# Hybrid SSD and attention layer: the first chunk's x and B transposed by TensorE instead of VectorE and DRAM

## The chip, the cores and the metric

The kernel runs on one core of a Trainium2 chip. The metric is device time in microseconds of one execution. The core's engines are TensorE (PE, with its weight loads as PEld), VectorE (DVE), ScalarE (ACT), GpSimd (POOL) and SyncE (SP); each works through its own queue of instructions in order and waits on semaphores set by the others. SyncE computes nothing here: it issues DMAs, in order too, and a DMA that has to wait holds back all that stand behind it.

## The reference

One decoder layer on 512 tokens of width 1024, in float32: a token mixer (a Mamba-2 SSD branch and a sliding-window attention branch from one input projection, merged by gates) and a SwiGLU FFN, with a layer norm around each. The change touches the chunked scan of the SSD branch alone. It has 32 heads of 64 in 4 groups of 8 heads, a state of 128, and 4 chunks of 128 tokens:

```python
X = (xh.astype(jnp.float32) * dt[..., None]).reshape(bsz, nc, T, ng, ne, hp)
Lmat = jnp.exp(segsum(dA))
CB = jnp.einsum('bclgn,bcsgn->bcgls', Cc, Bc)
y_diag = jnp.einsum('bcgels,bcsgep->bclgep', Lmat * CB[:, :, :, None], X)
decay_states = jnp.exp(a_cum[..., -1:] - a_cum)
states = jnp.einsum('bclgn,bcgel,bclgep->bcgepn', Bc, decay_states, X)
...
y_off = jnp.einsum('bclgn,bcgepn,bcgel->bclgep', Cc, h_in, jnp.exp(a_cum))
```

So each chunk needs X (x times dt), the decayed copy of X for the state, the state itself (B times decayed X, summed over the chunk's tokens), and two contributions to y: the diagonal one from L, CB and X, and the one from the state carried in.

## The kernel before

**Order.** TensorE's instructions stand in the order in which the code issues them (the schedule of TensorE is manual). Those of the other engines and the DMAs are put into their queues by a scheduler, so an edit can change their order at some distance. Pools give tiles a fixed number of buffers; an instruction that writes a tile whose buffer is still read waits.

**Products.** Every weight product is done in three matmuls per step of the contraction (`mm3`, L149 to L151): high times high, high times low, low times high. A weight tile arrives by DMA as `w_raw` (L120, four buffers), ScalarE rounds it to `w_hi` (L135) and VectorE makes the rest `w_lo` (L136), three buffers each, prepared up to three products ahead. A projection (`product`, L277) is 8 steps, 24 matmuls, into one of three PSUM accumulators `ps_mm`. It is a generator; `fill(us)` issues as many steps of the waiting generators as fit `us` at 0.65 us a step, with at most one step owed from before, and nothing when none is waiting.

**Stages.** First the input norm, and the projections of the attention branch with steps of others filled in; then attention; then products of the attention output. From 237 us the SSD stage runs: 16 turns i, four groups g of four chunks c. Its fill is the input projections of the next group (`g_xbc`, L357): a product, then a causal convolution in `evac`, one ScalarE instruction (L370) and three on VectorE (L373) that read the accumulator, then SiLU on ScalarE (L377).

**A turn of the SSD stage.** Everything lies with channels on the partitions, while X and B for the state are needed with tokens on the partitions.
- `ssd_pre(i)` (L739): SyncE loads the cumulative decays of the chunk from DRAM, broadcast to all partitions, into `L` (512 KB, three buffers, L745) and, for c > 0, `E` (L752). GpSimd masks L (L756) and ScalarE takes eight exponentials (L761).
- `ssd_x(i)` (L763): VectorE transposes x in blocks of 32 by 32 into `T` (four instructions, L770); SyncE writes T to DRAM (`t_d`, L774) and reads it back in the order that makes the transpose whole, into `R` (four DMAs, one buffer, L776). For c < 3 the same is done with B: `Tb` (one buffer, L781), `b_d` (L784), four reads into `bt` (L786).
- `ssd_dt(i)` (L790): VectorE multiplies R by dt into `X` (two instructions, L797), GpSimd multiplies X by the decays into `Xd` (two, L805).
- `ssd_a(i)` (L809): TensorE makes `ps_cb` from B and C (L822), ScalarE copies it to `cb` (L824), VectorE multiplies it into L (L826). At c = 0 ScalarE first writes `y_g` from x (four, L819).
- `ssd_b(i)` (L828): the state product `ps_st` from bt and Xd (L836), at c = 0 copied to `h_st` by ScalarE (L842), else added by VectorE (L848); for c > 0 the carried-in part `ps_yo` (L852); then, after a `fill`, the diagonal part `ps_yd` from X and L (L862), which VectorE adds to y (L864).

All PSUM tiles other than the three accumulators come from one pool of five buffers (`axt`).

**The start of the stage (L967 to L973).** Before the loop the code issues ssd_pre(0), ssd_pre(1), ssd_x(0), ssd_a(0), a fill, ssd_dt(0) and ssd_x(1). Turn 0 then adds the stage's projections to the fill queue (`add_stage`, L950) and issues ssd_pre(2), ssd_a(1), `fill(6.0)`, ps_st(0), ssd_dt(1), ssd_x(2), `fill(6.0)`, ps_yd(0), `fill(6.0)`.

Of the kernel before, what the change touches and what calls it, by code (L numbers as in the profile page):

```python
# [11 lines left out]
F32 = mybir.dt.float32  # L12
# [6 lines left out]
P = 128  # L19
# [43 lines left out]
def kernel(  # L63
# [13 lines left out]
    nc = tc.nc  # L77
# [3 lines left out]
    def pool(name, bufs=1, **kw):  # L81
        return tc.tile_pool(name=name, bufs=bufs, reuse_waits="tile", **kw)

    def gap(pl, size):
# [8 lines left out]
    ident = const.tile([P, P], F32, name="ident")  # L93
# [4 lines left out]
        out=tri, in_=tri, pattern=[[1, P]], compare_op=ALU.is_ge, fill=0.0,  # L98
# [54 lines left out]
    class Filler:  # L153
# [19 lines left out]
        def fill(self, us):  # L173
            self.owed += us / 0.65
            while self.owed >= 1.0 and self.step():
                self.owed -= 1.0
            self.owed = min(self.owed, 1.0)
# [91 lines left out]
    fill, need = filler.fill, filler.need  # L269

    def axt(shape, name):
        return psX.tile(shape, F32, name=name, tag="ax")

    def acc_tile(name):
        return psA.tile([P, S], F32, name=name, tag="mm")
# [79 lines left out]
    xbc_t = {}  # L355
# [184 lines left out]
    ps = [axt([P, S], "ps_dt"), axt([P, S], "ps_k"), acc_tile("ps_v"), acc_tile("ps_q")]  # L540
# [190 lines left out]
    sd = ssd_stack.enter_context(pool("ssd", side="right"))  # L731
# [5 lines left out]
    z_t, y_t, yn_t, L_t, E_t, R_t, X_t, Xd_t, bt_t, h_t = ({} for _ in range(10))  # L737

    def ssd_pre(i):  # L739

        g, c = divmod(i, NT)

        L = sd.tile([P, 2, 4, P], F32, name="L", tag="L", bufs=3)
        L_t[i] = L
        nc.sync.dma_start(  # L745
            out=L.rearrange("p j t l -> p j (t l)"),
            in_=ar[g, c].unsqueeze(0).broadcast_to([P, 2, 4 * P]))
        if c > 0:
            E = sd.tile([P, 4, P], F32, name="E", tag="E", bufs=2)
            E_t[i] = E  # L750
            for j in range(2):
                nc.sync.dma_start(  # L752
                    out=E[64 * j:64 * j + 64].rearrange("p t l -> p (t l)"),
                    in_=er[g, c, j].unsqueeze(0).broadcast_to([64, 4 * P]))
        Lf = L.rearrange("p j t l -> p (j t) l")
        nc.gpsimd.affine_select(  # L756
            out=Lf, in_=Lf, pattern=[[0, 8], [1, P]], compare_op=ALU.is_ge, fill=-BIG,
            base=0, channel_multiplier=-1)
        for j in range(2):
            for t in range(4):  # L760
                nc.scalar.activation(L[:, j, t], L[:, j, t], AF.Exp, bias=nac5[:, g, j, c, t:t + 1], scale=1.0)  # L761

    def ssd_x(i):  # L763

        g, c = divmod(i, NT)
        cs = slice(c * P, (c + 1) * P)

        T = sd.tile([P, 4, 4, 32], F32, name="T", tag="tmp", bufs=3)
        for t in range(4):
            nc.vector.transpose(T[:, :, t], xbc_t[g, 2 + t][:, cs])  # L770

        R = sd.tile([P, 4, 4, 32], F32, name="R", tag="R", bufs=1)
        R_t[i] = R
        nc.sync.dma_start(out=t_d[i], in_=T.rearrange("p b t s -> p b (t s)"))  # L774
        for b in range(4):
            nc.sync.dma_start(  # L776
                out=R[32 * b:32 * b + 32].rearrange("r a t s -> r a (t s)"),
                in_=t_d[i, :, b].rearrange("(a r) x -> r a x", r=32))
        if c < NT - 1:
            Tb = sd.tile([P, P], F32, name="Tb", tag="Tb", bufs=1)  # L780
            nc.vector.transpose(Tb, xbc_t[g, 0][:, cs])  # L781
            bt = sd.tile([P, P], F32, name="bt", tag="bt", bufs=2)
            bt_t[i] = bt
            nc.sync.dma_start(out=b_d[i], in_=Tb.rearrange("p (b s) -> p b s", b=4))  # L784
            for b in range(4):
                nc.sync.dma_start(  # L786
                    out=bt[32 * b:32 * b + 32].rearrange("r (a s) -> r a s", a=4),
                    in_=b_d[i, :, b].rearrange("(a r) s -> r a s", r=32))

    def ssd_dt(i):  # L790

        g, c = divmod(i, NT)
        R = R_t.pop(i)
        X = sd.tile([P, 4, 2, 64], F32, name="X", tag="X", bufs=2)
        X_t[i] = X
        for j in range(2):
            nc.vector.tensor_tensor(  # L797
                out=X[:, :, j].rearrange("p t (h s) -> p t h s", h=2),
                in0=R[:, 2 * j:2 * j + 2].rearrange("p h t s -> p t h s"),
                in1=dt5[:, g, j, c].unsqueeze(2).unsqueeze(3).broadcast_to([P, 4, 2, 32]), op=ALU.mult)  # L800
        if c < NT - 1:
            Xd = sd.tile([P, 4, 2, 64], F32, name="Xd", tag="Xd", bufs=1)
            Xd_t[i] = Xd
            for j in range(2):
                nc.gpsimd.tensor_tensor(  # L805
                    out=Xd[:, :, j], in0=X[:, :, j],
                    in1=dec5[:, g, j, c].unsqueeze(2).broadcast_to([P, 4, 64]), op=ALU.mult)

    def ssd_a(i):  # L809

        g, c = divmod(i, NT)
        cs = slice(c * P, (c + 1) * P)
        b_f, c_f = xbc_t[g, 0], xbc_t[g, 1]
        xs = [xbc_t[g, 2 + t] for t in range(4)]
        if c == 0:
            y = sd.tile([P, 4, S], F32, name="y_g", tag="y_g", bufs=1)
            y_t[g] = y
            for t in range(4):
                nc.scalar.mul(out=y[:, t], in_=xs[t], mul=pc[:, C_DS + 4 * g + t:C_DS + 4 * g + t + 1])  # L819
        L = L_t[i]  # L820
        ps = axt([P, P], "ps_cb")
        nc.tensor.matmul(ps, b_f[:, cs], c_f[:, cs], start=True, stop=True)  # L822
        cb = sd.tile([P, P], F32, name="cb", tag="cb", bufs=2)
        nc.scalar.copy(out=cb, in_=ps)  # L824
        Lf = L.rearrange("p j t l -> p (j t) l")
        nc.vector.tensor_tensor(out=Lf, in0=Lf, in1=cb.unsqueeze(1).broadcast_to([P, 8, P]), op=ALU.mult)  # L826
# [139 lines left out]

    ssd_pre(0)  # L967
    ssd_pre(1)
    ssd_x(0)
    ssd_a(0)  # L970
    fill(4.0)
    ssd_dt(0)
    ssd_x(1)  # L973
    norm = iter(())
    for i in range(NG * NT):
        g, c = divmod(i, NT)
# [13 lines left out]
        if i + 1 < NG * NT:  # L990
            ssd_dt(i + 1)
# [82 lines left out]
    for half in range(2):  # L1074
# [23 lines left out]
        for ti in toks:  # L1098
            hr = res[ti]
            for o in range(2):  # L1100
                os = slice(o * 512, (o + 1) * 512)
                nc.vector.scalar_tensor_tensor(
                    out=hr[:, os], in0=hr[:, os], scalar=ALPHA, in1=acc[ti][o], op0=ALU.mult, op1=ALU.add)
# [98 lines left out]
    for f in range(2, NF):  # L1202
        pss = []
        for u in (U_FG, U_FU):
            ps = psF.tile([P, S], F32, name="ps_ff", tag="mm")
# [23 lines left out]
    for cs in (slice(0, 256), slice(256, 512)):  # L1229
        ps = psD.tile([P, 256], F32, name="ps_end", tag="dn")  # L1230
# [74 lines left out]
```

## Time and profile before

| | |
|---|---|
| median of 3 runs | 1031.97 us (1031.74 to 1032.63) |
| the profiled execution | 1031.27 us |
| its span | 1029.5 us |
| TensorE busy | 1008.2 us, 98% of the span |
| VectorE, ScalarE, GpSimd busy | 616.8, 499.2, 207.4 us |
| mean granted clock of TensorE | 0.993 |

The span runs from the first to the last instruction; the rest of an execution's time lies around it. In rows of the timeline and of the chain the first two numbers are the start and the length in us; in brackets stands the idle time of the engine just before, and who ended it. Rows of the list of waits give total, count and longest. `x4` is a count of instructions. Matmuls overlap, so that a row's length is longer than the distance to the next start. A float32 matmul can be two records in the trace, hence `x2` at one ps_st and `x16` at the eight matmuls of one ps_yd.

### The profile page before, as it was taken

What the parts mean: (1) busy time and instruction counts of PE and PEld (TensorE: products, weight loads), DVE (VectorE), ACT (ScalarE), POOL (GpSimd) and SP (SyncE); (2) the same over time, 40 slices, a digit from 0 to 9 for tenths busy, and PEclk for the clock granted to TensorE, in tenths of its full rate; (3) what the DMA queues carried; (4) which work ended last, traced back from release to release, by engine and by line L of the source; (5) the groups of instructions that cost most, each with busy time, mean ns of one, the idle gap of its engine ahead of it and who ended that gap; (6) DMA issues with size and microseconds to landing.
All of it is one profiled execution on the core that took longest, in us unless ns stands there. A gap on an engine that the chain in (4) does not pass through costs nothing.

```text
span 1029.5 us, 13358 instructions
## 1 busy us (share of the span) xinstructions
PE 1008.2 (98%) x4968; PEld 830.0 (81%) x4968; DVE 616.8 (60%) x911; ACT 499.2 (48%) x848; POOL 207.4 (20%) x195
## 2 busy tenths in 40 slices
PE   8999999996999999999999999999999999999997
PEld 7888888884887887888888888898888888888886
DVE  6789874545655785696874585646433333332766
ACT  5464566716555786684652543334323332322441
POOL 2011223722204113212322820290000000000000
PEclk9999999998999999999999999999999999999999
DMA  8211223545554445445532344316433333331471
GB/s 316 82 62 62 88 83 106 198 146 148 171 156 146 153 153 151 125 142 159 166 113 83 115 150 180 107 42 225 144 122 114 111 111 114 123 123 62 147 251 53
DMA packets 58961, 136.53 MB, mean 133 GB/s; under 512 B 12912, under 2 KB 23152, under 8 KB 58640
## 3 DMA queue, kind: packets, MB, share of 16 engines
q1 hardware_dynamic: 56240, 126.11, 37.9%
q0 software_dynamic: 2080, 7.47, 2.0%
q10 hardware_dynamic: 576, 2.10, 0.5%
q8 instruction: 39, 0.64, 0.3%
q14 instruction: 26, 0.21, 0.1%
HBM read 124.25 MB, written 11.40 MB: 132 GB/s over the span
## 4 chain that ended last, share of the span: by engine, by line
PE 88%; DVE 4%; ACT 3%; DMA 3%; issue 1%; POOL 1%; SPq 0%; ACTq 0%; POOLq 0%; DVEq 0%
PE ps_mm L149 13%; PE ps_mm L150 13%; PE ps_mm L151 13%; PE ps_ff L151 8%; PE ps_ff L149 8%; PE ps_ff L150 8%; PE ps_da L151 2%; PE ps_da L149 2%; PE ps_da L150 2%; PE ps_db L150 2%; PE ps_db L151 2%; PE ps_db L149 2%; PE ps_mix L149 1%; PE ps_mix L151 1%; PE ps_mix L150 1%; DMA L<-a_d 1%
## 5 line engine op out<-in xcount | busy, mean ns | idle before, releaser
L136 DVE TENSOR_TENSOR w_lo<-w_raw,w_hi 128x1024 fp32r<-128x1024 f32 x185 | 241.3, 1309 | 171.1 <-ACT w_hi L135 169.0
L135 ACT CAST w_hi<-w_raw 128x1024 fp32r<-128x1024 f32 x185 | 193.6, 1050 | 307.9 <-PE ps_ff L150 124.4
L149 PE MATMUL ps_mm<-hT_hi,w_hi 128*128 128x512 f32 x504 | 204.3, 405 | 0.7 <-DVE cacc L373 0.7
L150 PE MATMUL ps_mm<-hT_lo,w_hi 128*128 128x512 f32 x504 | 197.2, 391 | 0.0
L151 PE MATMUL ps_mm<-hT_hi,w_lo 128*128 128x512 f32 x504 | 197.0, 391 | 0.0
L149 PE MATMUL ps_ff<-h2T_hi,w_hi 128*128 128x512 f32 (+1 forms) x384 | 143.3, 373 | 0.0
L151 PE MATMUL ps_ff<-h2T_hi,w_lo 128*128 128x512 f32 (+1 forms) x384 | 142.6, 371 | 0.0
L150 PE MATMUL ps_ff<-h2T_lo,w_hi 128*128 128x512 f32 (+1 forms) x384 | 142.6, 371 | 0.0
L149 PEld LDWEIGHTS ps_mm<-hT_hi,w_hi 128*128 128x128 f32 x504 | 95.0, 188 | 23.2 <-issue 4.2
L151 PEld LDWEIGHTS ps_mm<-hT_hi,w_lo 128*128 128x128 f32 x504 | 94.8, 188 | 20.6
L150 PEld LDWEIGHTS ps_mm<-hT_lo,w_hi 128*128 128x128 f32 x504 | 95.1, 189 | 18.7 <-issue 1.2
L150 PEld LDWEIGHTS ps_ff<-h2T_lo,w_hi 128*128 128x128 f32 x384 | 72.3, 188 | 12.6
L151 PEld LDWEIGHTS ps_ff<-h2T_hi,w_lo 128*128 128x128 f32 x384 | 72.3, 188 | 12.5
L149 PEld LDWEIGHTS ps_ff<-h2T_hi,w_hi 128*128 128x128 f32 x384 | 72.3, 188 | 12.4
L1152 DVE TENSOR_TENSOR sgf<-sgf,ps_ff 128x512 f32<-128x512 f32 x22 | 15.1, 685 | 68.3 <-PE ps_ff L151 68.3
L149 PE MATMUL ps_mm<-yh,w_hi 128*128 128x512 f32 x124 | 49.4, 399 | 0.3 <-ACT yacc L934 0.3
L150 PE MATMUL ps_mm<-yl,w_hi 128*128 128x512 f32 x124 | 48.4, 390 | 0.0
L151 PE MATMUL ps_mm<-yh,w_lo 128*128 128x512 f32 x124 | 48.3, 390 | 0.0
L756 POOL TENSOR_SCALAR_AFFINE_SELECT L<-L 128x1024 f32<-128x1024 f32 x16 | 21.8, 1360 | 118.2 <-DMA L<-a_d 92.5
L761 ACT ACTIVATE L<-L,nac 128x128 f32<-128x128 f32 x128 | 40.1, 390 | 6.9 <-POOL L L756 6.6
L373 DVE SCALAR_TENSOR_TENSOR cacc<-ps_mm,pc,cacc 128x511 f32<-128x511 f32 (+2 forms) x54 | 39.6, 737 | 6.2 <-ACT cacc L370 5.7
L150 PE MATMUL ps_da<-w_lo,hA_hi 128*128 128x512 f32 x88 | 34.2, 389 | 0.0
(264 smaller groups left out, 1675.4 us busy)
## 6 DMA issues: line engine op xcount, KB each, us to landing
w_raw<-in_wall_dram SPq DMA_DIRECT2D x187, 512.0 KB, 3.4
L<-a_d SPq DMA_DIRECT2D x16, 512.0 KB, 5.9
t_d<-T SPq DMA_DIRECT2D x16, 256.0 KB, 3.9
R<-t_d SPq DMA_DIRECT2D x64, 64.0 KB, 2.0
E<-e_d SPq DMA_DIRECT2D x24, 128.0 KB, 3.5
x_d<-x_sb POOLq DMA_DIRECT2D x4, 512.0 KB, 7.8
row<-x_d POOLq DMA_DIRECT2D x4, 512.0 KB, 5.1
h_d<-row POOLq DMA_DIRECT2D x4, 512.0 KB, 3.0
```

The costliest lines, as they stand in the source:

```text
L135: (copy or nc.scalar.copy)(out=hi, in_=w)
L136: self.last = (eng or nc.vector).tensor_sub(out=lo, in0=w, in1=hi.bitcast(F32))
L149: nc.tensor.matmul(ps, lh, rh, start=start, stop=False)
L150: nc.tensor.matmul(ps, lh, rl, start=False, stop=False)
L151: nc.tensor.matmul(ps, ll, rh, start=False, stop=stop)
L373: nc.vector.scalar_tensor_tensor(out=acc[:, d:], in0=ps[:, :S - d], scalar=pc[:, cw + 3 - d:cw + 4 - d], in1=acc[:, d:], op0=ALU.mult, op1 ...
L756: nc.gpsimd.affine_select(out=Lf, in_=Lf, pattern=[[0, 8], [1, P]], compare_op=ALU.is_ge, fill=-BIG, base=0, channel_multiplier=-1)
L761: nc.scalar.activation(L[:, j, t], L[:, j, t], AF.Exp, bias=nac5[:, g, j, c, t:t + 1], scale=1.0)
L1152: nc.vector.tensor_mul(sg, sg, pu)
```

## The change

x and B of turn 0 are no longer transposed by `ssd_x(0)`. A new function `ssd_first` transposes them on TensorE, by matmuls with the identity, four 128 by 128 blocks of x into one PSUM tile `ps_x` and one of B into `ps_bt`. `R_t[0]` is now a view of `ps_x`, so that `ssd_dt(0)` reads PSUM; `bt` is copied from `ps_bt` by ScalarE. `ssd_a(0)` comes first, the new function behind it, and the fill that stood ahead of `ssd_dt(0)` now stands behind `ssd_x(1)`. All other turns are as before.

```diff
+    def ssd_first():
+
+        ps = axt([P, 4, P], "ps_x")
+        for t in range(4):
+            nc.tensor.transpose(ps[:, t], xbc_t[0, 2 + t][:, 0:P], ident)
+        R_t[0] = ps.rearrange("p t (a s) -> p a t s", a=4)
+        ps = axt([P, P], "ps_bt")
+        nc.tensor.transpose(ps, xbc_t[0, 0][:, 0:P], ident)
+        bt_t[0] = sd.tile([P, P], F32, name="bt", tag="bt", bufs=2)
+        nc.scalar.copy(out=bt_t[0], in_=ps)
...
     ssd_pre(0)
     ssd_pre(1)
-    ssd_x(0)
     ssd_a(0)
-    fill(4.0)
+    ssd_first()
     ssd_dt(0)
     ssd_x(1)
+    fill(4.0)
```

Eleven lines are added, so that lines from 790 on have numbers higher by 11 after the change (X is L797 before and L808 after).

VectorE's queue at the start of the SSD stage, before. The numbers in the names tell tiles of one name apart: T_2367 and Tb_2276 are of chunks 2 and 1, L_2201 and L_2214 of chunks 0 and 1, X_2259 and X_2361 of chunks 0 and 1; cacc_2337 is the first projection's convolution.

```order
L781 STREAM_TRANSPOSE Tb_2276<-bc_f_612 128x128
L826 TENSOR_TENSOR L_2201<-L_2201,cb_2256 128x1024
L826 TENSOR_TENSOR L_2214<-L_2214,cb_2302 128x1024
L373 SCALAR_TENSOR_TENSOR cacc_2337<-ps_mm_2306,pc_79,cacc_2337 128x511
L136 TENSOR_TENSOR w_lo_2348<-w_raw_2130,w_hi_2347 128x1024
L797 TENSOR_TENSOR X_2259<-R_2235,dtv_97 128x4x64 x2
L373 SCALAR_TENSOR_TENSOR cacc_2337<-ps_mm_2306,pc_79,cacc_2337 128x510
L373 SCALAR_TENSOR_TENSOR cacc_2337<-ps_mm_2306,pc_79,cacc_2337 128x509
L781 STREAM_TRANSPOSE Tb_2378<-bc_f_612 128x128
L797 TENSOR_TENSOR X_2361<-R_2270,dtv_97 128x4x64 x2
```

The same queue after, from the stage's first instruction on. T and Tb without numbers are of chunk 1, then of chunk 2; the first X is of chunk 0, the second of chunk 1.

```order
L770 STREAM_TRANSPOSE T<-xs_f 128x4x32
L808 TENSOR_TENSOR X<-ps_x,dtv 128x4x64 x2
L770 STREAM_TRANSPOSE T<-xs_f 128x4x32 x3
L781 STREAM_TRANSPOSE Tb<-bc_f 128x128
L136 TENSOR_TENSOR w_lo<-w_raw,w_hi 128x1024
L770 STREAM_TRANSPOSE T<-xs_f 128x4x32 x4
L781 STREAM_TRANSPOSE Tb<-bc_f 128x128
L837 TENSOR_TENSOR L<-L,cb 128x1024 x2
L808 TENSOR_TENSOR X<-R,dtv 128x4x64 x2
L373 SCALAR_TENSOR_TENSOR cacc<-ps_mm,pc,cacc 128x511
L373 SCALAR_TENSOR_TENSOR cacc<-ps_mm,pc,cacc 128x510
L136 TENSOR_TENSOR w_lo<-w_raw,w_hi 128x1024
```

X of chunk 0 has moved from behind the second Tb, both L products, a convolution step and a w_lo to second place; X of chunk 1 now stands ahead of the first projection's convolution.

ScalarE's queue from y_g on, before:

```order
L819 ACTIVATE y_g<-xs_f,pc 128x512 x4
L824 COPY cb<-ps_cb 128x128 x2
L761 ACT_TABLE_LOAD
L761 ACTIVATE L<-L,nac 128x128 x16
L370 ACTIVATE cacc<-ps_mm,pc 128x512
L135 CAST w_hi<-w_raw 128x1024
L761 ACTIVATE L<-L,nac 128x128 x8
L377 ACT_TABLE_LOAD
```

And after:

```order
L830 ACTIVATE y_g<-xs_f,pc 128x512 x4
L835 COPY cb<-ps_cb 128x128
L799 COPY bt<-ps_bt 128x128
L835 COPY cb<-ps_cb 128x128
L761 ACT_TABLE_LOAD
L761 ACTIVATE L<-L,nac 128x128 x24
L370 ACTIVATE cacc<-ps_mm,pc 128x512
L135 CAST w_hi<-w_raw 128x1024
```

The exponentials of three chunks instead of two now stand ahead of the first projection's convolution (L370) and of the weight rounding for the fourth projection (L135).

On TensorE the five transposes stand between ps_cb of chunk 0 and ps_cb of chunk 1, which stood side by side; behind them its order is as it was. On GpSimd the two Xd of chunk 0 have moved from behind three masks of L (L756) to ahead of them. On SyncE the ten DMAs of chunk 0 (t_d, four R, b_d, four bt) are gone, the third L stands directly behind t_d and b_d of chunk 1, and t_d and b_d of chunk 2 stand behind the next w_raw.

## The prediction

> **What bounds the kernel now.** I read the page first, then the list of TensorE's own waits, then the stretch around the longest wait.
>
> ```profile
> span 1029.5 us, 13358 instructions
> PE 1008.2 (98%) x4968; PEld 830.0 (81%) x4968; DVE 616.8 (60%) x911; ACT 499.2 (48%) x848; POOL 207.4 (20%) x195
> ...
> PEclk9999999998999999999999999999999999999999
> ```
>
> ```profile
> PE ps_st L836 <- POOL Xd L805: 10.0, 1, 10.0
> PE ps_warm L547 <- POOL ident masks.py:199: 1.5, 1, 1.5
> PE ps_mm L149 <- DVE cacc L373: 0.7, 1, 0.7
> ```
>
> TensorE is busy 98% of the span, so work hidden beside it is worth nothing; only its waits and its own instructions are. One wait stands out: once in the program, the state product ps_st of chunk 0 waits 10.0 us for Xd from GpSimd. All other waits are under 2 us, and the clock row has, besides the last, one slice of 40 under 0.9, the tenth (231.6 to 257.4), where that wait lies. The same place cut into stages (columns: length, busy time of PE, PEld, DVE, ACT, POOL, then the granted clock, DMA share, GB/s):
>
> ```profile
> 237.00:244.70 7.70, 7.67 (x36) 6.08 (x34) 4.36 (x15) 5.56 (x10) 1.09 (x1) 1.00 0.79 163
> 244.70:254.64 9.94, 0.00 (x1) 0.00 (x1) 6.40 (x9) 8.48 (x25) 4.27 (x4) 0.67 0.55 170
> 254.64:263.63 8.99, 8.99 (x29) 6.36 (x29) 2.39 (x5) 4.11 (x5) 2.37 (x4) 0.79 0.70 193
> ```
>
> The stall is in the second row, and in the third the clock comes back only at 0.79: the wait costs more than its own length. Who made Xd late is in the chain of waits and in the queues of VectorE and SyncE:
>
> ```profile
> 241.43 5.92 DMA b_d<-Tb
> ...
> 253.29 1.30 POOL Xd L805 x2
> 254.64 2.08 PE ps_st L836 x2
> ```
>
> ```profile
> 240.50 0.83 SPq L774 DMA_DIRECT2D t_d<-T  x1
> 242.87 0.48 SPq L745 DMA_DIRECT2D L<-a_d  x1
> 247.47 1.75 SPq L776 DMA_DIRECT2D R<-t_d  x4
> ```
>
> ```profile
> 247.70 0.31 DVE L781 STREAM_TRANSPOSE Tb<-bc_f 128x128 f32<-128x128 f32 x1 [5.89 <-DMA b_d<-Tb]
> 247.93 1.18 DVE L826 TENSOR_TENSOR L<-L,cb 128x1024 f32<-128x1024 f32 x1
> ```
>
> Chunk 0's transposed x goes out at 240.50 and is fetched back only from 247.47; VectorE meanwhile stands before the Tb of chunk 1, whose single buffer is free when chunk 0's b_d has landed, and X(0), the product that needs R(0), is queued behind that, two L products, a conv step and a w_lo. X(0) runs at 252.8, Xd(0) until 254.6.
>
> **The change part by part.**
>
> *Removed: the wait.* X(0) now comes from TensorE's transposes, without DRAM. The price of the wait and of the ramp behind it:
>
> ```profile
> 238.16 0.39 PE L151 MATMUL ps_mm<-hT_hi,w_lo 128*128 128x512 f32 x1
> 244.28 0.39 PE L151 MATMUL ps_mm<-hT_hi,w_lo 128*128 128x512 f32 x1
> 254.64 2.08 PE L836 MATMUL ps_st<-Xd,bt 128*128 128x512 f32 x2 [9.97 <-POOL Xd L805]
> 263.63 1.09 PE L862 MATMUL ps_yd<-L,X 128*64 128x128 f32 x16
> 264.66 0.50 PE L149 MATMUL ps_mm<-hT_hi,w_hi 128*128 128x512 f32 x1
> ```
>
> ```profile
> 277.46 0.86 PE ps_st L836 x2
> ```
>
> The idle time is 9.97 us. At full clock 27 matmuls take 244.28 - 238.16 = 6.12 us, and a ps_st that doesn't wait takes 0.86 (the next chunk's, in the chain). From ps_st to ps_yd stand just these, one ps_st and 27 matmuls (9 steps of 3): 6.98 us at full clock, against 263.63 - 254.64 = 8.99. The ramp costs 2.01 us and goes with the wait. [...] The trace has 2.01, and that is what I use.
>
> *Added on TensorE.* Five transposes. The nearest row is eight like them in the chain:
>
> ```profile
> 64.55 0.87 PE ps_pt L479 x8
> ```
>
> That is 0.109 each, 0.54 for five, all on the path. The bounds are nothing (if TensorE has a gap there) and twice that (if they overlap less, behind other shapes); I take the row. [...]
>
> *Is ps_st(0) then ready in time?* TensorE comes to it at 244.51 + 0.54 = 245.05 (244.28 plus one spacing of 0.23). VectorE and ScalarE:
>
> ```profile
> 238.05 0.88 DVE L770 STREAM_TRANSPOSE T<-xs_f 128x128 f32<-128x128 f32 x4
> 252.79 0.75 DVE L797 TENSOR_TENSOR X<-R,dtv 128x256 f32<-128x256 f32 x2
> ```
>
> ```profile
> 240.64 0.40 ACT L824 COPY cb<-ps_cb 128x128 f32<-128x128 f32 x2
> ```
>
> VectorE is free for its first transpose at 238.05; one (0.2) is ahead of X(0), X(0) takes 0.75 and GpSimd, which is idle, 1.3: about 240.5. That X reads PSUM in another order isn't in the trace; even at twice the 0.75 it is 241.3. bt(0) is one more copy like cb's, behind the first of them: about 241.2. Both are some 4 us early. The 0.75 on VectorE takes the place of chunk 0's five block transposes, 1.1 us. The two new PSUM tiles come from five that rotate; the next to take their places are ps_cb of chunk 2 and ps_st(1), long after X and the copy have read them. The fill that is moved finds an empty queue before and now, since the stage's projections are added later: ten steps stay ahead of ps_st(0), nine behind it.
>
> *Moved on SyncE.* Ten DMAs fewer: t_d, b_d, 4 R, 4 bt. Chunk 1's take chunk 0's place in the queue, at the same times, since t_d(1) and b_d(1) still stand behind two L and two E. So Tb of chunk 2 runs at 247.7 as Tb of chunk 1 did, and L(0)'s product ends at 249.1 (247.93 + 1.18). TensorE needs it for ps_yd(0) at 245.05 + 0.86 + 6.12 = 252.0: early by 2.9 us. R(1) is fetched from 247.5; ps_st(1) comes 13.7 us after ps_yd(0) (263.63 to 277.3) and doesn't wait for it. Chunk 2's t_d and R now stand behind weight loads that wait for w_lo, R(2) behind that of P3 (about 256, below); ps_st(2) comes a chunk later still.
>
> *What is late next: the fourth projection of this stage.* TensorE has three accumulators for projections, so the fourth (call them P0 to P3) waits for P0's conv steps, and its weights for w_hi and w_lo. It is reached after ps_yd(0), 252.0 + 1.03 (263.63 to 264.66), and the 5 steps of P2 that are left, 15 x 0.227 = 3.4: 256.5. On ScalarE, P0's conv start L370 and w_hi now stand behind all 24 exponentials, so behind L(2) and its DMA. Sixteen selects on GpSimd (ns minimum, median, maximum), and the rows of this place:
>
> ```profile
> L756 POOL TENSOR_SCALAR_AFFINE_SELECT L<-L x16: 1086/1092/2158, 243.0 to 511.8; 128x1024 f32<-128x1024 f32 x16
> ```
>
> ```profile
> 249.91 1.89 POOL L756 TENSOR_SCALAR_AFFINE_SELECT L<-L 128x1024 f32<-128x1024 f32 x1 [2.86 <-DMA L<-a_d]
> 251.83 2.45 ACT L761 ACTIVATE L<-L,nac 128x128 f32<-128x128 f32 x8 [0.70 <-POOL L L756]
> 249.44 0.76 ACT L370 ACTIVATE cacc<-ps_mm,pc 128x512 f32<-128x512 f32 x1
> 251.42 1.45 DVE L136 TENSOR_TENSOR w_lo<-w_raw,w_hi 128x1024 fp32r<-128x1024 f32 x1
> 253.47 1.52 DVE L373 SCALAR_TENSOR_TENSOR cacc<-ps_mm,pc,cacc 128x510 f32<-128x510 f32 x2
> ```
>
> L(2) landed at 249.9. One t_d (256 KB, 1.5 us at the 170 GB/s of the stage row) and 0.5 us of issue stand ahead of it no more: 247.9 to 249.9, I take 248.7. From landing: select 1.5 (1.89 here, median 1.09), exponentials 2.45, L370 0.76, then two conv steps 1.5, w_lo 1.45, and the last conv step 0.75: 8.4 us, so 257.1. P3 waits 0.6 us; the bounds are 0 (landing at 247.9, select 1.09: 255.9) and 2.3 (249.9 and 1.89: 258.7).
>
> **The sum.** The profiled execution took 1031.27 us, 1.77 outside its span and 0.70 below the median of the runs shown. 1031.27 - 9.97 - 2.01 + 0.54 + 0.6 = 1020.4; with 0.70 for the median, **1021.1 us**.
>
> **The rivals.**
> *A, the wait moves to P3.* For it: ScalarE's order above, and the 0.7 us wait for cacc in the first list is of just this kind. Against it: fewer DMAs ahead of L(2). With the whole 2.3 and no loss of clock 1031.97 - 11.98 + 0.54 + 2.3 = 1022.8; with a ramp of 2.0 again 1024.8. The rows show a ramp behind 9.97 us and, by the clock row, none behind 0.7. [...]
>
> *B, a later stage takes half back.* At the change of group, from 315, the chain leaves TensorE for a DMA, GpSimd, ScalarE and VectorE; its first step:
>
> ```profile
> 314.14 1.02 PE ps_yd L862 x16
> ...
> 315.60 7.46 DMA L<-a_d
> ```
>
> If that chain kept its old time, TensorE would come 11 us early and wait. Against it: the L DMA starts right behind ps_yd, so the chain moves with TensorE. If half is lost, 1026.5.
>
> *C, the change doesn't do what it says*: ps_st(0) still waits, for a reason that the trace of before can't show (X held by a buffer). Then about 1031.
>
> *D, slower.* The same P3, but L(2) so late that its wait exceeds the gain. P3 waits for landing + 8.4 - 256.5; the gain without it is 11.4; so it decides from a landing at 259.5, 17 us after the issue at 242.87. At 262 the time is 1031.97 - 11.4 + 13.9 = 1034.5. Against it: the L loads' time to landing, minimum, median, maximum.
>
> ```profile
> DMA to landing us min/median/max: 4.7/5.9/8.0
> ```
>
> **How the numbers follow.** About 0.2% (2.1 us) is what a measurement of this kernel can tell from no change. Forecast (P3 waits under 1 us) 0.70, A 0.17, B 0.06, C 0.04, D 0.03. Forecast, A and B are faster by over 0.2%: 0.93; C is within: 0.04; D slower: 0.03. The range begins at 1019.3: no wait at P3 gives 1020.5, and the small waits and the profiled run's 0.7 below the median may take another 1.2. It ends at 1025.5: A with the ramp, 1024.8, and 0.7 of small waits further on.
>
> **What would show it.** Right: no wait of ps_st for Xd; the clock at 1.00 between 237 and 265; ps_yd(0) at about 252.0 instead of 263.6; P3's first matmul at about 257.1 with a short wait for cacc L373. The step on the transposes is wrong if P0 starts later than 238.2 by more than 0.5; the step on L(2) if P3 waits over 2.3 us. The whole is wrong if ps_st(0) still waits, or if the 11 us gained by 265 are gone by the first ps_yd of the next group.

## The result and the profile after

| | before | after |
|---|---|---|
| median, both timed in turn | 1031.86 us (1031.68 to 1032.63) | 1020.50 us (1020.22 to 1020.75) |
| the profiled execution | 1031.27 us | 1020.6 us |
| its span | 1029.5 us | 1018.9 us |
| mean granted clock | 0.993 | 0.998 |

The change makes the kernel faster: the ratio is 0.9888, with a 95% interval of 0.9871 to 0.9906. The forecast was 1021.1 us, 0.6 above the measured median. The page of after:

```profile
span 1018.9 us, 13347 instructions
PE 1006.8 (99%) x4973; PEld 829.3 (81%) x4973; DVE 619.5 (61%) x906; ACT 498.7 (49%) x849; POOL 209.8 (21%) x195
...
PEclk9999999999999999999999999999999999999999
```

TensorE has five records more (the transposes), VectorE five fewer (the block transposes that are gone), and no slice of the clock row is below 9 any more. (In the row of before only the tenth slice is; the last, which the prediction excepts, is a 9 there too.) TensorE's own waits in after, those from the SSD stage on:

```profile
PE ps_mm L149 <- DVE cacc L373: 0.9, 1, 0.9
...
PE ps_mm L149 <- ACT z L881: 0.4, 1, 0.4
PE ps_mm L149 <- ACT yacc L945: 0.3, 1, 0.3
```

The 10 us of ps_st are gone, and no wait of like size has taken their place. What is left are three waits of under 1 us, all later in the program; two of them, for cacc and yacc, were there before with 0.7 and 0.3 us, and the one for z is new. The place of the change, cut at ps_st(0) (same columns as in the prediction):

```profile
237.00:244.95 7.95, 7.95 (x42) 6.71 (x41) 4.38 (x13) 6.46 (x14) 2.27 (x3) 1.00 0.80 192
244.95:252.06 7.11, 7.11 (x30) 5.25 (x28) 3.42 (x5) 6.51 (x22) 3.59 (x4) 1.00 0.48 145
```

Before, three rows stood here, and the middle one was the stall. Now TensorE is busy in all of it, at a clock of 1.00. TensorE's timeline in after, first the place of the change and then the three later waits:

```profile
237.12 0.38 PE L833 MATMUL ps_cb<-bc_f 128*128 128x128 f32 x2
237.34 0.60 PE L794 MATMUL ps_x<-ident,xs_f 128*128 128x128 f32 x4
237.78 0.27 PE L797 MATMUL ps_bt<-ident,bc_f 128*128 128x128 f32 x1
...
238.03 0.48 PE L149 MATMUL ps_mm<-hT_hi,w_hi 128*128 128x512 f32 x1
...
244.95 1.02 PE L847 MATMUL ps_st<-Xd,bt 128*128 128x512 f32 x2
252.06 1.09 PE L873 MATMUL ps_yd<-L,X 128*64 128x128 f32 x16
256.62 0.39 PE L149 MATMUL ps_mm<-hT_hi,w_hi 128*128 128x512 f32 x1
...
323.43 0.47 PE L149 MATMUL ps_mm<-hT_hi,w_hi 128*128 128x512 f32 x1 [0.91 <-DVE cacc L373]
355.36 0.50 PE L149 MATMUL ps_mm<-hT_hi,w_hi 128*128 128x512 f32 x1 [0.36 <-ACT z L881]
381.94 0.50 PE L149 MATMUL ps_mm<-yh,w_hi 128*128 128x512 f32 x1 [0.34 <-ACT yacc L945]
```

The five transposes stand right behind the first ps_cb; P0 starts at 238.03. ps_st(0) starts at 244.95 with nothing in brackets, where it started at 254.64 before. ps_yd(0) starts at 252.06, against 263.63: 11.57 us earlier, of which 0.13 lie ahead of the change (the first ps_cb starts at 237.12 instead of 237.25). The row at 256.62 is the first matmul of P3, and it doesn't wait. On VectorE, GpSimd and ScalarE in after, the work that had to be in time:

```profile
238.15 0.72 DVE L808 TENSOR_TENSOR X<-ps_x,dtv 128x256 f32<-128x256 f32 x2
...
255.00 1.40 DVE L373 SCALAR_TENSOR_TENSOR cacc<-ps_mm,pc,cacc 128x509 f32<-128x509 f32 x2
```

```profile
238.63 1.18 POOL L816 TENSOR_TENSOR Xd<-X,dec 128x256 f32<-128x256 f32 x2 [26.61 <-DVE X L808]
247.96 1.26 POOL L756 TENSOR_SCALAR_AFFINE_SELECT L<-L 128x1024 f32<-128x1024 f32 x1 [1.57 <-DMA L<-a_d]
```

```profile
240.65 0.26 ACT L799 COPY bt<-ps_bt 128x128 f32<-128x128 f32 x1
```

X(0) now runs at 238.15 instead of 252.79, and Xd(0) is done at 239.8, bt(0) at 240.9: four to five us ahead of ps_st(0). L(2) has landed when its select starts, at 247.96. The two conv steps from 255.00 on are the last of P0's, which ends at about 255.7, and one of P1's.

### The profile page after: what moved, and what is told of

Its sections match the earlier page's. It is cut to its first block, busy times and chain, and to the rows that moved or that the text cites. A ratio compares the mean times of both kernels' runs of the same rounds, so it can differ in the third digit from the quotient of the medians.

```text
span 1018.9 us, 13347 instructions
## 1 busy us (share of the span) xinstructions
PE 1006.8 (99%) x4973; PEld 829.3 (81%) x4973; DVE 619.5 (61%) x906; ACT 498.7 (49%) x849; POOL 209.8 (21%) x195
## 4 chain that ended last, share of the span: by engine, by line
PE 91%; DMA 3%; DVE 3%; ACT 1%; POOL 1%; issue 1%; SPq 0%; POOLq 0%; ACTq 0%; DVEq 0%
PE ps_mm L149 14%; PE ps_mm L150 14%; PE ps_mm L151 14%; PE ps_ff L151 8%; PE ps_ff L149 8%; PE ps_ff L150 8%; DMA L<-a_d 2%; PE ps_da L151 2%; PE ps_da L149 2%; PE ps_da L150 2%; PE ps_db L151 2%; PE ps_db L150 2%; PE ps_db L149 2%; PE ps_mix L149 1%; PE ps_mix L151 1%; PE ps_mix L150 1%
## 5 line engine op out<-in xcount | busy, mean ns | idle before, releaser
L135 ACT CAST w_hi<-w_raw 128x1024 fp32r<-128x1024 f32 x185 | 193.5, 1050 | 300.7 <-PE ps_ff L150 125.4
L150 PEld LDWEIGHTS ps_ff<-h2T_lo,w_hi 128*128 128x128 f32 x384 | 72.3, 188 | 12.6
L756 POOL TENSOR_SCALAR_AFFINE_SELECT L<-L 128x1024 f32<-128x1024 f32 x16 | 20.4, 1278 | 84.0 <-DMA L<-a_d 71.0
L149 PE MATMUL ps_da<-w_hi,hA_hi 128*128 128x512 f32 x88 | 34.2, 389 | 0.0
```

Source lines behind the costliest of these rows:

```text
L135: (copy or nc.scalar.copy)(out=hi, in_=w)
L149: nc.tensor.matmul(ps, lh, rh, start=start, stop=False)
L150: nc.tensor.matmul(ps, lh, rl, start=False, stop=False)
L756: nc.gpsimd.affine_select(out=Lf, in_=Lf, pattern=[[0, 8], [1, P]], compare_op=ALU.is_ge, fill=-BIG, base=0, channel_multiplier=-1)
```

## The experiments

The theory on trial: ps_st(0) needs two transposed inputs, both came late by way of DRAM, and TensorE's transposes make both early; what is gained is the stall and the clock ramp behind it, what is paid is five transposes. The rivals: one of the two inputs alone does it; not the transposes but the lighter queues of SyncE and VectorE do it; the queue of VectorE alone, blocked by Tb, does it; a transpose costs more than the row of eight says. All medians are beside the kernel before in the same series, which had 1031.5 to 1032.2 us. The edits are shown against the kernel after, except where the text starts from the kernel before or from the kernel with all chunks by TensorE; `...` marks lines left out.

| kernel | median (range), us | ratio to before, 95% |
|---|---|---|
| x alone by TensorE | 1026.93 (1026.42 to 1028.03) | 0.9941 to 0.9970 |
| B alone by TensorE | 1031.50 (1030.29 to 1031.98) | 0.9986 to 1.0005 |
| before, Tb unblocked | 1029.93 (1029.27 to 1031.24) | 0.9975 to 0.9994 |
| before, TensorE kept busy | 1030.53 (1029.47 to 1033.07) | 0.9977 to 0.9998 |
| after, old trip kept | 1022.25 (1021.49 to 1022.87) | 0.9894 to 0.9924 |
| all chunks by TensorE | 1033.04 (1030.01 to 1036.01) | 0.9999 to 1.0025 |
| the same, shared PSUM tile | 1035.35 (1032.93 to 1037.44) | 1.0015 to 1.0042 |
| the same, cb copied by VectorE | 1026.79 (1025.67 to 1027.07) | 0.9937 to 0.9964 |
| after, early trip for x | 1019.91 (1018.48 to 1021.38) | 0.9872 to 0.9902 |
| after, once more | 1020.41 (1020.07 to 1021.14) | 0.9869 to 0.9898 |
| early trip, once more | 1019.68 (1018.73 to 1020.05) | 0.9859 to 0.9889 |
| after, cb copied by VectorE | 1023.29 (1021.00 to 1024.41) | 0.9899 to 0.9930 |

### x alone

x of chunk 0 by TensorE, B by VectorE and DRAM as before.

```diff
-        ps = axt([P, P], "ps_bt")
-        nc.tensor.transpose(ps, xbc_t[0, 0][:, 0:P], ident)
-        bt_t[0] = sd.tile([P, P], F32, name="bt", tag="bt", bufs=2)
-        nc.scalar.copy(out=bt_t[0], in_=ps)
+        Tb = sd.tile([P, P], F32, name="Tb", tag="Tb", bufs=1)
+        nc.vector.transpose(Tb, xbc_t[0, 0][:, 0:P])
+        bt = sd.tile([P, P], F32, name="bt", tag="bt", bufs=2)
+        bt_t[0] = bt
+        nc.sync.dma_start(out=b_d[0], in_=Tb.rearrange("p (b s) -> p b s", b=4))
+        for b in range(4):
+            nc.sync.dma_start(
...
```

> Half of the change: x of chunk 0 is transposed by TensorE, B still goes through VectorE and DRAM. Theory (the state product waits for the later of Xd(0) and bt(0), and the wait has a clock ramp behind it): b_d now goes out at about 240.5, lands some 6 us later, four bt reads take 1.8 us to issue and 1.8 to land, so bt(0) is there at about 250 and TensorE, which comes at 244.9, waits some 5 us and loses 1 to 2 us of clock: about 1027 us, between 1025 and 1029. Rival 1 (the gain came from the DRAM traffic taken away): x is 80% of those bytes, so about 1023. Rival 2 (the gain came from X(0) leaving its place behind Tb in VectorE's queue): all of it stays, about 1020.5.

Measured 1026.93 us. TensorE at ps_st(0), and the DMA that it waits for in SyncE's queue:

```profile
250.11 2.04 PE L852 MATMUL ps_st<-Xd,bt 128*128 128x512 f32 x2 [5.13 <-DMA bt<-b_d]
```

```profile
246.36 1.75 SPq L802 DMA_DIRECT2D bt<-b_d  x4
```

With x early, the same matmul waits 5.1 us for B. So B's trip was late as well, hidden behind x's. x alone brings under half of the gain.

### B alone

B by TensorE, x by VectorE and DRAM as before.

```diff
-        ps = axt([P, 4, P], "ps_x")
+        T = sd.tile([P, 4, 4, 32], F32, name="T", tag="tmp", bufs=3)
         for t in range(4):
-            nc.tensor.transpose(ps[:, t], xbc_t[0, 2 + t][:, 0:P], ident)
-        R_t[0] = ps.rearrange("p t (a s) -> p a t s", a=4)
+            nc.vector.transpose(T[:, :, t], xbc_t[0, 2 + t][:, 0:P])
+        R = sd.tile([P, 4, 4, 32], F32, name="R", tag="R", bufs=1)
+        R_t[0] = R
+        nc.sync.dma_start(out=t_d[0], in_=T.rearrange("p b t s -> p b (t s)"))
+        for b in range(4):
+            nc.sync.dma_start(
...
```

> The other half: B of chunk 0 is transposed by TensorE, x still goes through VectorE and DRAM. Theory: Xd(0) is as late as before, since R(0) is fetched from about 247.5 and X(0) still stands behind the L products, a conv step and a w_lo on VectorE: the wait of ps_st(0) is 9 to 10 us and the time 1030.5 to 1032. Rival 1 (traffic): B is 20% of the bytes, about 1029.7. Rival 2 (X(0) behind Tb): X(0) stays behind a Tb here, about 1031.5.

Measured 1031.50 us, no difference. TensorE and VectorE there:

```profile
253.63 2.08 PE L854 MATMUL ps_st<-Xd,bt 128*128 128x512 f32 x2 [9.46 <-POOL Xd L823]
```

```profile
251.78 0.75 DVE L815 TENSOR_TENSOR X<-R,dtv 128x256 f32<-128x256 f32 x2
```

X(0) runs only 1.0 us earlier than in before (252.79), and ps_st(0) waits for Xd almost as long. Of the 1.0 us, 0.64 are the whole place starting earlier (the first ps_cb at 236.61 instead of 237.25). From there to ps_yd(0) this execution takes 27.11 us, 0.73 more than before, because the clock's ramp is longer (3.0 us, last section). The two gains are not a sum: x alone brings 4.8 us, B alone 0.2, which is within the noise, both 11.4. ps_st(0) has two late inputs and starts with the later one: with x early it waits 5.13 us for bt, with B early 9.46 us for Xd.

### Tb unblocked

The kernel before, but chunk 0's Tb gets a tile of its own, so that VectorE need not stand before the Tb of chunk 1.

```diff
-            Tb = sd.tile([P, P], F32, name="Tb", tag="Tb", bufs=1)
+            if i == 0:
+                Tb = sd.tile([P, S], F32, name="z", tag="z", bufs=4)[:, 0:P]
+            else:
+                Tb = sd.tile([P, P], F32, name="Tb", tag="Tb", bufs=1)
```

> The kernel before, with Tb of chunk 0 in a buffer of its own (one of z's, unused at that time), so that Tb of chunk 1 does not wait on VectorE for b_d of chunk 0. Nothing is transposed by TensorE. Theory: R(0) lands at 250 to 251 whatever VectorE does, and the scheduler puts X(0) behind both L products and one conv step still; only a w_lo leaves its way: ps_st(0) starts 1 to 1.5 us earlier, about 1030.5, between 1029.3 and 1031.9. Rival 2 (the wait was VectorE standing before Tb): most of the gain without any transpose on TensorE, below 1024.

Measured 1029.93 us. TensorE, VectorE and SyncE's queue:

```profile
252.68 2.08 PE L839 MATMUL ps_st<-Xd,bt 128*128 128x512 f32 x2 [8.29 <-POOL Xd L808]
```

```profile
250.83 0.75 DVE L800 TENSOR_TENSOR X<-R,dtv 128x256 f32<-128x256 f32 x2
```

```profile
246.66 1.75 SPq L776 DMA_DIRECT2D R<-t_d  x4
```

The wait falls by 1.7 us and the time by 1.6 to 1.8. The blocked buffer, the most striking link of the chain in the profile, was worth no more. Without it X(0) follows an L product and a conv step on VectorE with no gap, so the trace doesn't name its data as what it waited for. But SyncE fetches R(0) only from 246.66 to 248.41, and X(1) of this kernel has its data 1.6 us behind the end of such a fetch; by that, an estimate, R(0) was whole at about 250.0, and X(0) could have started 0.8 us sooner at most.

### TensorE kept busy

The kernel before, with 44 matmuls ahead of ps_st(0) whose result nobody reads; they fill the stall.

```diff
+            if i == 0:
+                idle = axt([P, S], "ps_idle")
+                for _ in range(44):
+                    nc.tensor.matmul(idle, ones_r, hT_hi[:, 0], start=True, stop=True)
             pss = axt([P, 4, 2, 64], "ps_st")
```

> The kernel before, with 44 matmuls of 128x512 whose result nobody reads put ahead of ps_st(0): TensorE is busy for about 10 us where it was idle, and ps_st(0) starts when it did. It takes the ramp by itself. Theory (2.0 us of the 12 are the clock coming back after the idle time): no ramp behind, 1031.9 - 2.0 = 1029.9 us, between 1029.3 and 1030.5. Rival (the slow stretch behind the wait has another cause, such as loads or accumulators that come late): 1031.9, and 27 matmuls behind ps_st(0) still take 8 us.

Measured 1030.53 us, 0.03 above the expected range. The place in two stages:

```profile
245.00:255.00 10.00, 10.00 (x45) 8.11 (x44) 6.11 (x9) 8.79 (x26) 4.14 (x4) 1.00 0.59 180
255.00:264.00 9.00, 9.00 (x50) 6.73 (x49) 4.14 (x7) 4.12 (x5) 2.70 (x5) 1.00 0.68 178
```

ps_st(0) comes as late as before (at 255.36, 17.49 us behind the first ps_cb against 17.39), but the clock behind it is 1.00, and ps_yd(0) follows 7.16 us later instead of 8.99. So the ramp is a cost of its own, 1.83 us here. By the medians the whole program keeps 1.2 of it. The profiled execution, with 1031.71 us the second slowest of ten, keeps nothing: in its list of waits a later one has grown, from 0.28 us in before.

```profile
PE ps_mm L149 <- ACT yacc L938: 2.0, 1, 2.0
```

What lengthened it, and whether the faster executions have it too, was not followed up.

### The old trip kept

After, but chunk 0's block transposes and its ten DMAs are still made; nobody reads what they bring.

```diff
     ssd_dt(0)
+    used = bt_t[0]
+    ssd_x(0)
+    R_t.pop(0)
+    bt_t[0] = used
     ssd_x(1)
```

> The changed kernel, and beside it chunk 0's old path is still walked: five block transposes on VectorE, ten DMAs to DRAM and back, whose result nobody reads. Theory (what counts is when Xd(0) and bt(0) are ready, not the traffic): ps_st(0) does not wait, 1020.5 us, between 1019.8 and 1022.0; the third L lands later again, so P3 may wait up to 1.5 us. Rival (the gain comes from the traffic, the DMA issue and the VectorE work taken away): they are all back, so about 1031.

Measured 1022.25 us, 0.25 above the expected range. Nearly the whole gain is there, so it doesn't come from lighter queues. The 1.75 us that are missing are not lost at the place of the trip: from ps_cb(0) to ps_yd(0) this kernel takes the same 14.94 us as after. They are lost some 120 us later. From the list of TensorE's waits, and SyncE's queue of this kernel at that place:

```profile
PE ps_mm L149 <- ACT w_hi L135: 1.4, 1, 1.4
PE ps_mm L151 <- DVE w_lo L136: 0.7, 1, 0.7
```

```profile
347.04 0.33 SPq L774 DMA_DIRECT2D t_d<-T  x1
347.46 0.39 SPq L745 DMA_DIRECT2D L<-a_d  x1
```

And the same two rows of SyncE's queue in after:

```profile
345.22 0.39 SPq L745 DMA_DIRECT2D L<-a_d  x1
346.97 0.33 SPq L774 DMA_DIRECT2D t_d<-T  x1
```

The scheduler has set a t_d ahead of the L of the second chunk of group 1. L goes out 2.2 us later, ScalarE's exponentials come 2.5 us later, and a w_hi that stands behind them makes TensorE wait at 364. That this order is the cause is read from the queues; no kernel put back the order alone.

### All chunks by TensorE

All 16 chunks as the change treats the first: 76 transposes, none by VectorE and DRAM.

```diff
-    def ssd_first():
+    def ssd_pe(i):
...
-            nc.tensor.transpose(ps[:, t], xbc_t[0, 2 + t][:, 0:P], ident)
+            nc.tensor.transpose(ps[:, t], xbc_t[g, 2 + t][:, cs], ident)
...
-    ssd_x(1)
...
+            ssd_pe(i + 1)
             ssd_dt(i + 1)
...
-            ssd_x(i + 2)
```

> All 16 chunks by TensorE: 60 more transposes of x and 11 more of B, each chunk's just ahead of its X; VectorE's block transposes and all DMAs of t_d and b_d are gone. Theory: no other chunk waited, so there is nothing more to gain, and 71 transposes at 0.109 cost 7.7 us: 1028.2, between 1026.5 and 1029.5; the lower part if VectorE and SyncE, freed of 15 us of work and 150 DMAs, end the waits of 1.6 us at the changes of group. Rival (traffic and VectorE's work cost the time): faster than the changed kernel, below 1020. [...]

Measured 1033.04 us: a miss, 5 us above the expected time. TensorE, one stage, and ScalarE in this kernel:

```profile
341.47 0.33 PE L800 MATMUL ps_bt<-ident,bc_f 128*128 128x128 f32 x1 [3.19 <-ACT cb L838]
```

```profile
341.47:345.00 3.53, 3.53 (x10) 2.76 (x11) 3.53 (x4) 1.73 (x3) 0.00 (x0) 0.54 0.01 2
345.00:350.24 5.24, 5.24 (x24) 4.36 (x23) 5.20 (x9) 4.81 (x5) 3.36 (x4) 0.98 0.51 152
```

```profile
339.28 1.28 ACT L761 ACT_TABLE_LOAD   x1
340.57 0.69 ACT L761 ACTIVATE L<-L,nac 128x128 f32<-128x128 f32 x2
341.17 0.24 ACT L838 COPY cb<-ps_cb 128x128 f32<-128x128 f32 x1
```

One ps_bt got the PSUM buffer in which a ps_cb still waited to be copied, and that copy stood behind exponentials and table loads on ScalarE. The wait is 3.19 us, and behind it the clock was 0.54 for 3.5 us and 0.98 for 5.2: 1.6 + 0.1 = 1.7. With 71 x 0.109 = 7.7 that makes 12.6 us; the kernel is 12.5 above after. So close a fit is partly chance: this execution also lacks 0.8 us of after's later waits, and the ten runs spread from 1030.0 to 1036.0 us. Two experiments put this to the test.

### A shared PSUM tile

As the last, but B's transpose goes into the second half of ps_cb's tile.

```diff
-            ps = axt([P, P], "ps_bt")
-            nc.tensor.transpose(ps, xbc_t[g, 0][:, cs], ident)
+            ps = cb_t.pop(i)
+            nc.tensor.transpose(ps[:, 1], xbc_t[g, 0][:, cs], ident)
...
-        ps = axt([P, P], "ps_cb")
+        ps = axt([P, 2, P], "ps_cb")
+        cb_t[i] = ps
+        ps = ps[:, 0]
```

> All 16 chunks by TensorE as in the run before it, but the transposed B goes into the second half of ps_cb's PSUM tile instead of a sixth kind of tile in the rotation of five. Theory (the 71 transposes cost 0.109 us each as in the forecast, and the rest of the excess was one wait of 3.2 us of ps_bt for the buffer of a ps_cb whose copy stood behind other work on ScalarE, and a clock ramp of 1.7 us behind it): 1020.5 + 7.7 = 1028.2 us, range 1027.0 to 1029.9, no wait of ps_bt in the list of TensorE's waits. Rival (a transpose is dearer among other work than the row of eight says, about 0.18 us): still about 1033, with the same time at the chunks but no long wait. Rival (ScalarE's order is what holds, and the wait turns up at another matmul, such as ps_x or ps_st): 1031 to 1033 with a new wait of about 3 us.

Measured 1035.35 us: another miss, and a faulty experiment. TensorE and two stages:

```profile
241.46 0.33 PE L802 MATMUL ps_cb<-ident,bc_f 128*128 128x128 f32 x1 [2.86 <-ACT cb L842]
...
343.32 0.33 PE L802 MATMUL ps_cb<-ident,bc_f 128*128 128x128 f32 x1 [2.95 <-ACT cb L842]
```

```profile
241.46:248.70 7.24, 7.24 (x34) 6.03 (x34) 1.23 (x1) 6.00 (x17) 2.19 (x2) 1.00 1.00 255
...
343.32:350.36 7.04, 7.04 (x32) 5.81 (x33) 7.04 (x10) 4.83 (x7) 2.31 (x4) 1.00 0.24 77
```

The transpose now waits for the copy of its own tile's other half, the same copy on ScalarE, and does so twice. The edit had not removed the suspect but tied the matmul to it. The sum is 1020.4 + 7.7 + 2.9 + 3.0 = 1034.0, and no ramp: the clock behind both waits is 1.00. That is near the profiled execution, which took 1033.55 us; the median is 1.4 above the sum. The six runs reach from 1032.9 to 1037.4 us, and the mean granted clock is 0.998 in the profiled one and 0.993 in the slowest, so in other executions the same waits may have cost clock; that isn't shown.

### The copy of cb by VectorE

As "All chunks by TensorE", with one more line.

```diff
-        nc.scalar.copy(out=cb, in_=ps)
+        nc.vector.tensor_copy(out=cb, in_=ps)
```

> All 16 chunks by TensorE, B's transposed block in a PSUM tile of its own as in the first such run, but the copy of ps_cb is made by VectorE instead of ScalarE, so that it doesn't stand behind exponentials, y_g or table loads. Theory (beyond 71 transposes at 0.109 us only that copy cost anything: 3.2 us and a ramp of 1.7): 1020.4 + 7.7 = 1028.1 us, range 1027.0 to 1029.9, no wait of ps_bt in the list of TensorE's waits and no clock under 1.00 at 341 to 350 us. Rival (a transpose is dearer among other work, about 0.18 us): 1033. Rival (VectorE's queue holds the copy as ScalarE's did, behind conv steps and w_lo): a wait of 1 to 3 us in another place, 1029.5 to 1033.

Measured 1026.79 us, 0.21 below the expected range: 6.2 us under the kernel without this line, and 5 under before. The same ps_bt, and a stage around it:

```profile
336.99 0.27 PE L800 MATMUL ps_bt<-ident,bc_f 128*128 128x128 f32 x1
```

```profile
337.00:345.00 8.00, 8.00 (x45) 6.44 (x45) 6.14 (x9) 4.50 (x7) 2.37 (x4) 1.00 0.27 87
```

No wait, clock 1.00. The waits for cacc, z and yacc, 1.6 us in after, are not in this kernel's list either. Above after it is 1026.79 - 1020.41 = 6.4 us; with the 1.6 that it saves, 8.0 us for 71 transposes: 0.112 each, against 0.109 from the row of eight; without that credit it is 0.090. Both are far from the rival's 0.18. That a transpose is dearer among other work has fallen. It also shows where the change stops paying: for chunks whose DRAM trip nobody waits for, a transpose on TensorE is a plain cost, 0.09 to 0.11 us each here.

### An early trip for x

After, but x of chunk 0 goes by way of DRAM, started some 40 us ahead of the stage in two buffers that are free then; B by TensorE.

```diff
+    T, early = (ph1.tile([P, S], F32, name="cacc", tag="cacc", bufs=2) for _ in range(2))
...
+    for t in range(4):
+        nc.vector.transpose(T[:, :, t], xbc_t[0, 2 + t][:, 0:P])
+    nc.sync.dma_start(out=t_d[0], in_=T.rearrange("p b t s -> p b (t s)"))
+    for b in range(4):
+        nc.sync.dma_start(
...
-            nc.tensor.transpose(ps[:, t], xbc_t[0, 2 + t][:, 0:P], ident)
...
+        R_t[0] = early
```

> x of chunk 0 goes through VectorE and DRAM as before the change, but starts some 40 us earlier, under the products of the attention output, in the two buffers of cacc that are unused then; B of chunk 0 by TensorE as in the change. The traffic is that of before, the four transposes of x on TensorE are gone. Theory (only the time of the trip counted): no wait of ps_st(0), and 4 x 0.109 = 0.44 less than the changed kernel: 1020.1 us, between 1019.3 and 1021.5. Rival (traffic): about 1030. Rival (a DRAM trip on SyncE's queue always costs, here by holding back weight loads): a wait for weights among the products before 237, 1021.5 or more.

Measured 1019.91 us. To set it beside after, both were run once more, together:

> The changed kernel once more, for a comparison on the same chip with the run of the early trip: 1020.5 us, range 1019.9 to 1021.2.

> The early trip (x of chunk 0 through VectorE and DRAM some 40 us ahead of the stage, B by TensorE) once more beside the changed kernel. Theory (only the four transposes of x are saved on the path, 4 x 0.109 = 0.44 us): 0.4 us under the changed kernel of the same call, range 0.0 to 0.9. Rival (the small waits at the changes of group absorb it): no difference, within 0.2. Rival (the early DMAs and VectorE work delay attention): slower by 0.3 or more.

Measured 1020.41 (1020.07 to 1021.14) and 1019.68 (1018.73 to 1020.05). The difference is 0.73 us; the ranges of the four runs of each don't overlap, but nearly touch, and the early trip's first four runs reach up to 1021.38. So it is at the edge of what these runs can tell. TensorE in the second run of the early trip:

```profile
237.50 0.38 PE L840 MATMUL ps_cb<-bc_f 128*128 128x128 f32 x2
...
252.01 1.09 PE L880 MATMUL ps_yd<-L,X 128*64 128x128 f32 x16
```

From ps_cb(0) to ps_yd(0) are 14.51 us, against 14.94 in after: 0.43 less, four transposes at 0.109. So for x it is the earliness that counts, not the engine: a trip through DRAM that starts in time does as well, and is cheaper by TensorE's share. The other 0.3 us may lie in the small waits later on, which this profile doesn't have. That isn't shown: the profile is of the fastest of the four runs, and the first profile of the same kernel has a wait of 1.2 us there.

### After, with cb copied by VectorE

The line that helped above, in after.

```diff
-        nc.scalar.copy(out=cb, in_=ps)
+        nc.vector.tensor_copy(out=cb, in_=ps)
```

> The changed kernel with one more edit: VectorE copies ps_cb to cb instead of ScalarE, in all 16 turns. Theory (what the change gives back at the changes of group, 0.9, 0.4 and 0.3 us of waits for cacc, z and yacc, comes from ScalarE's queue there, and goes when ScalarE has 16 copies fewer; the run with all chunks on TensorE and this copy on VectorE showed none of these waits): 1020.4 - 1.6 = 1018.8 us, range 1018.2 to 1019.7. Rival (the order that the scheduler happens to find decides, not ScalarE's load): about 1020.4, within 0.5, with waits of about the same sum in other places. Rival (VectorE's conv steps come later, and the wait for cacc at P3 or at the changes of group grows): 1021 to 1023.

Measured 1023.29 us: a miss with the wrong sign. TensorE, the stage behind the wait, and SyncE's queue ahead of it:

```profile
362.76 0.50 PE L149 MATMUL ps_mm<-hT_hi,w_hi 128*128 128x512 f32 x1 [1.31 <-ACT w_hi L135]
...
364.31 0.50 PE L151 MATMUL ps_mm<-hT_hi,w_lo 128*128 128x512 f32 x1 [0.82 <-DVE w_lo L136]
```

```profile
364.31:368.50 4.19, 4.19 (x22) 3.06 (x23) 3.66 (x8) 3.68 (x6) 0.00 (x0) 0.59 0.82 222
```

```profile
345.93 0.33 SPq L774 DMA_DIRECT2D t_d<-T  x1
346.35 0.39 SPq L745 DMA_DIRECT2D L<-a_d  x1
```

Up to 340 the theory held: ps_ms of the first group (L902, sums of squares of its y) starts at 340.13 instead of 341.24, and the waits for cacc, z and yacc are gone. Then the scheduler sets t_d ahead of L, just as in the kernel with the old trip kept, and a w_hi is late again: 2.1 us of waits and a ramp of 4.19 x 0.41 = 1.7. In before, after, the kernels with x alone, B alone, Tb unblocked and TensorE kept busy, and that with the early trip, L goes out ahead of this t_d, and none of them has this wait for w_hi. The expectation had taken a line that helped in one program for one that helps in every program. In the kernel with all chunks on TensorE there is no t_d that could go ahead of L.

## Why the prediction was right

**The wait.** The forecast took off 9.97 us; ps_st(0) doesn't wait. Idle time counts from the end of a matmul's record. By starts it was 254.64 - 244.51 = 10.13 us, which makes up for what the ramp below lacks. X(0) was forecast for about 240.5 with Xd, bt(0) for 241.2; they were ready at 239.8 and 240.9. Reading ps_x in another order costs X nothing that shows (0.72 against 0.75 us for the two).

**The ramp.** 2.01 us were taken off. From ps_st(0) to ps_yd(0) after takes 7.11 us at full clock, so it was 8.99 - 7.11 = 1.88; the experiment that kept TensorE busy has 1.83. The last section shows other stalls here that cost up to 3.0.

**The transposes.** 0.54 us were added. P0 starts 0.91 us behind ps_cb(0), against 0.36 without the transposes: 0.55. The records last 0.27 us each, but they start 0.11 us apart (the four of ps_x from 237.34 on, ps_bt at 237.78), and it is the starts that TensorE's time is made of.

**P3.** This term was mis-sized: 0.6 us were added, and P3 doesn't wait. L(2) landed at 247.96, at the low end of 247.9 to 249.9, and from there to the end of P0's last conv step (255.70) went 7.7 us, not 8.4. It was done 0.9 us ahead of P3 (256.62). The cover is thin, but it held.

**What was left out.** From the first ps_cb to ps_yd(0) the gain is 26.38 - 14.94 = 11.44 us, just the 9.97 + 2.01 - 0.54 of the forecast. The forecast kept it to the end. With the 0.13 ahead of the change it is 11.57 us at ps_yd(0) and still so at the first ps_yd of the next group (317.81 against 329.38), 11.40 at the first ps_ms (341.24 against 352.64), and 10.7 from 382 on to the end: about 0.9 go between 318 and 382, in the turns of the second group. The waits in the list explain 0.6 of it: cacc 0.91 instead of 0.73, z 0.36 that is new, yacc 0.34 instead of 0.28. That is rival B, at well under a fifth of its size. Why these stages take part of the gain back was narrowed down (ScalarE's and SyncE's queues there, by the last experiment), but the edit made to remove these waits brought another. They also change from one execution of a kernel to the next: after has 0.5, 0.5 and 0.3 us of them in its second profile, the early trip 1.2 us in its first and none in its second.

**How near the total came.** For the profiled execution the forecast was 1020.4 us, and 1020.6 were measured: the 0.9 lost later and the 0.6 at P3 nearly cancel, two errors of opposite sign. The other term that was off is the 0.70 us for the median. It was taken from before, where the profiled execution lay that far below the median; the profiled execution of after lies 0.1 above its own. This is where the 0.6 us between 1021.1 and 1020.5 come from. The mechanism and the large terms were right; that the total is as near as this is in part luck.

**The other rivals.** C fell, since ps_st(0) doesn't wait. D needed a landing after 259.5; it came 11.5 us ahead of that. A fell with P3's missing wait.

## What to carry to other kernels

Where one instruction waits for two inputs, look up when each would be there: the profile names only the later, and mending one alone may bring nothing (B alone brought 0.2 us here, within the noise). Count the ramp of the clock with the stall, since the four stalls of 5.13 to 9.97 us each had one here, of 1.9 to 3.0 us, and price small matmuls by the distance of their starts (0.11 us for a transpose here) and not by the length of their records (0.27). Where a scheduler orders the queues, an edit of nothing but cheap work can move the time at a distance, here by 1.75 us some 120 us further on: look there before crediting or blaming the edit.

## What the runs showed of the hardware

In these runs the price of a ramp doesn't follow from the length of the stall. By the distance from ps_st(0) to ps_yd(0) over the 7.11 us that after takes at a clock of 1.00 it was, in one execution each, 1.88 us behind 9.97 idle (before), 1.9 behind 8.29 (Tb unblocked), 2.8 behind 5.13 (x alone) and 3.0 behind 9.46 (B alone). One wait of 3.19 us (all chunks by TensorE) cost 1.7, two waits of 2.86 and 2.95 us (the shared PSUM tile) cost no clock at all, and 1.31 and 0.82 us, with two matmuls between them (after, cb copied by VectorE), cost 1.7. The kernel with the old trip kept has nearly the same pair at the same place, 1.45 and 0.72 us, and lost no clock behind it:

```profile
365.46:370.00 4.54, 4.54 (x31) 3.51 (x31) 3.87 (x8) 4.51 (x8) 0.00 (x0) 1.00 0.75 216
```

So a like wait cost the ramp in one execution and not in the other.

What stands ahead of such a wait doesn't tell them apart either. With cb copied by VectorE, TensorE was idle for 2.13 of the 2.86 us ahead of 364.31, and the clock behind was 0.59 for 4.19 us; with the old trip kept it was idle for 2.17 of the 2.90 us ahead of 365.46, also with two matmuls between, and the clock stayed at 1.00. Four transposes stand right ahead of the waits of 2.86, 2.95 and 3.19 us, and only the last cost clock: 0.54 for 3.53 us behind it, against 1.00 for 7.24 and 7.04 us behind the others. What starts a ramp here, and what sets its price, isn't shown.
